# Seven block products instead of eight in part of a feed-forward input product, with PSUM kept as two tiles of four banks

## The chip, the cores and the metric

The kernel runs on one core of a Trainium2 chip, as one program. The metric is the device time of one execution in microseconds (us). The engines that matter are TensorE (PE in the profile; its weight loads are PEld), VectorE (DVE), ScalarE (ACT), and SyncE (SP), which issues the loads.

## The reference, cut to what matters

The model is a decoder trunk of two layers on 256 tokens with 2048 features, all in float32. Layer 0 has a recurrent block, layer 1 a sliding window attention, and each has a feed-forward part behind it:

```python
def swiglu_ffn(x, g, w_in, w_out):
    h = rms_norm(x, g)
    gate, up = jnp.split(h @ w_in, 2, axis=-1)
    return x + (jax.nn.silu(gate) * up) @ w_out
...
        if layer < N_REC:
            x = recurrent_block(x, norm1_g[layer], ...)
        else:
            if layer == N_REC:
                k_band, v_band = shared_kv(x, kv_norm_g, w_kv, k_norm_g)
            x = attn_block(x, norm1_g[layer], w_q[j], q_norm_g[j], sinks[j], w_o[j], k_band, v_band)
        x = swiglu_ffn(x, norm2_g[layer], ffn_w_in[layer], ffn_w_out[layer])
```

`w_in` of a feed-forward part (FFN) is 2048 x 11264 (gate and up, 5632 columns each), `w_out` 5632 x 2048.

## The kernel before

The residual stream `x` lies in SBUF for the whole program, with features on the 128 partitions and tokens in columns. All of the program is one stream of 704 chunks of weights (`stream`, L246). A chunk is 256 rows of a weight matrix by 512 of its columns, 128 partitions x 1024 numbers, 512 KB. At step i SyncE issues the load of chunk i + 4 into one of four buffers `raw`, chunk i + 3 is split, and the products of chunk i are issued.

A float32 product is made of three faster ones. `split` (L238) rounds a chunk to `hi` (ScalarE, L243) and takes the rest `lo` = raw − hi (VectorE, L244). Activations are split in the same way into a slot of 512 columns, 256 high and 256 low (there are 58 slots, L77). The products are hi x high, hi x low and lo x high.

`group` (L275) makes 512 output columns: four PSUM banks, one for each 128 columns, gather over all chunks of the group. `products` (L263, with the matmul on L271) issues 24 matmuls of 128x128 weights by 256 tokens for a chunk; in chunks 0, 2 and 5 (`SYNC`) three pairs of them are joined into matmuls of 512 columns, high and low side by side in the bank. The eight PSUM banks are eight tiles `b0` to `b7` (L83). `bank` (L163) takes one from the front of a queue, `free_bank` (L166) puts it at the back when its last read has been issued.

The order of the chunks, by number: 0 to 71 the input product and gates of the recurrent block in the order of `ORDER` (L53: x and y are groups of eight chunks, g is one chunk of gates, L547), 72 to 103 its output product, 104 to 279 the input product of FFN 0 (22 groups of 8), 280 to 367 its output product, 368 to 375 keys and values, 376 to 407 queries (L932, with tokens in rows), 408 to 439 the output product of the attention, 440 to 615 and 616 to 703 the two products of FFN 1. In the attention stage, work on heads is mixed among these chunks: scores (L783), their reads by a custom VectorE instruction (L794), transposes (L828, L906), values (L847).

What follows a group is issued by generator functions. `done` of a group reads its banks at once (`pull`, L306), tasks do the rest. `run_bg` (L194) steps the tasks at half a chunk, as long as an account of VectorE and ScalarE time (`self.dve`, `self.act`; each half tick takes 640 and 800 ns off) allows it. The helpers `a` (ScalarE, L107), `tt` (VectorE, L116) and `stt` (L120) record nearly all of these instructions, so their lines stand for many uses.

In `ffn` (L416) a group has 256 gate and 256 up columns. The product runs on x times the gain; the norm's factor `rstd` is multiplied on when the banks are read. A task then applies Silu, multiplies gate by up and splits the result into a slot `hid`, which `project` (L409) multiplies by `w_out`; `residual` (L387) adds the result to `x`.

## Time and profile before

| what | value |
|---|---|
| median of three runs | 2002.42 us (2001.57 to 2002.87) |
| the profiled execution | 2001.9 us |
| its span | 2000.1 us |
| TensorE busy, matmuls | 1991.9 us, 16509 instructions |
| VectorE busy | 1278.1 us, 2047 instructions |
| ScalarE busy | 1077.0 us, 1612 instructions |
| loaded from memory | 371.86 MB |

The profile is that of one execution. The span is the time from its first to its last instruction on the core. In rows of groups, out<-in names the tiles with their buffer numbers left out (`b` is any PSUM bank, `s` any slot, `h` a half buffer of 256 columns), then follow partitions x elements, the count, the busy time, the mean of one in ns, the idle time ahead of them and what ended it. Timeline rows have a start in us, a duration in us, engine, line, operation and count. A matmul's end is modelled; the starts are the better measure of what TensorE does.

### The profile page before, as it was taken

Reading aid. Unit: us, or ns where it says so; the run is one execution under the profiler, and the core shown is the slowest. Engines: PE = TensorE matmul, PEld = TensorE weight load, DVE = VectorE, ACT = ScalarE, POOL = GpSimd, SP = SyncE. Lnnn points to the kernel's source line nnn. Section 1 sums busy time; section 2 is a strip of 40 time slices with the busy share of each in tenths; the row PEclk is TensorE's granted clock in tenths of the full one; section 3 lists DMA queues with packets and bytes.
Section 4 is the critical chain, followed back from the end, with each engine's and each line's share of the span. In section 5 each row is a group of like instructions: output and inputs, shape, how many; then the busy total and the mean of one; then the engine's idle time right before and its main releaser. Section 6 shows DMA issues by size and latency. Waiting matters only on the chain. (4 is left out here: it accounts for less than half of the span.)

```text
span 2000.1 us, 39673 instructions
## 1 busy us (share of the span) xinstructions
PE 1991.9 (100%) x16509; PEld 1938.3 (97%) x16509; DVE 1278.1 (64%) x2047; ACT 1077.0 (54%) x1612; POOL 0.2 (0%) x4
## 2 busy tenths in 40 slices
PE   9999999999999999999999999999999999999999
PEld 9999999999999999999998789999999999999999
DVE  8989867556556655545677776765565566554443
ACT  7798655445445444444556775554454454444432
POOL 0000000000000000000000000000000000000000
PEclk9999999999999999999999999999999999999999
DMA  7554555555555555555554334555555555555553
GB/s 276 191 182 179 206 193 189 194 197 191 195 195 191 195 195 191 196 193 195 196 180 150 114 127 150 189 195 195 191 191 199 195 196 190 194 196 202 207 203 128
DMA packets 105012, 376.54 MB, mean 188 GB/s; under 512 B 11648, under 2 KB 13824, under 8 KB 104832
## 3 DMA queue, kind: packets, MB, share of 16 engines
q1 hardware_dynamic: 104544, 373.60, 52.3%
q8 instruction: 129, 2.11, 0.4%
q10 hardware_dynamic: 288, 0.40, 0.1%
q14 instruction: 51, 0.42, 0.1%
HBM read 371.86 MB, written 2.10 MB: 187 GB/s over the span
## 5 line engine op out<-in xcount | busy, mean ns | idle before, releaser
L271 PE MATMUL b<-s,hi 128*128 128x256 f32 (+1 forms) x9947 | 1356.4, 283 | 1.6 <-ACT s L107 1.2
L244 DVE TENSOR_TENSOR lo<-raw,hi 128x1024 fp32r<-128x1024 f32 (+1 forms) x705 | 860.9, 1222 | 669.1 <-ACT hi L243 666.1
L271 PEld LDWEIGHTS b<-s,hi 128*128 128x128 f32 x9947 | 1256.0, 188 | 26.2 <-ACT s L107 2.0
L243 ACT ACTIVATE hi<-raw 128x1024 fp32r<-128x1024 f32 (+1 forms) x705 | 746.1, 1059 | 773.0 <-PE b L271 728.1
L271 PE MATMUL b<-s,lo 128*128 128x256 f32 x5248 | 781.2, 276 | 0.0
L271 PEld LDWEIGHTS b<-s,lo 128*128 128x128 f32 x5248 | 680.7, 188 | 0.1
L932 PE MATMUL b<-hi,s 128*128 128x512 f32 x256 | 84.0, 408 | 0.0
L107 ACT ACTIVATE t<-b 128x256 f32<-128x256 f32 x122 | 45.9, 384 | 60.7 <-PE b L271 36.1
L932 PEld LDWEIGHTS b<-hi,s 128*128 128x128 f32 x256 | 45.8, 189 | 9.6 <-issue 1.4
L107 ACT ACTIVATE s<-b 128x256 fp32r<-128x256 f32 (+4 forms) x98 | 41.6, 465 | 19.5 <-PE b L828 7.9
L932 PE MATMUL b<-lo,s 128*128 128x512 f32 x128 | 50.8, 396 | 0.0
L107 ACT ACTIVATE h<-h 128x256 f32<-128x256 f32 (+1 forms) x104 | 38.9, 375 | 20.9 <-DVE h L116 20.8
L107 ACT ACTIVATE s<-h 128x256 fp32r<-128x256 f32 (+1 forms) x106 | 42.7, 413 | 13.1 <-DVE h L116 10.7
L116 DVE TENSOR_TENSOR h<-b,rstd 128x256 f32<-128x256 f32 x102 | 41.6, 415 | 0.0
L107 ACT ACTIVATE s<-x,par 128x256 fp32r<-128x256 f32 x80 | 37.8, 498 | 2.8 <-DVE x L116 1.8
L116 DVE TENSOR_TENSOR h<-h,rstd 128x256 f32<-128x256 f32 x92 | 38.3, 420 | 1.5
L107 ACT ACT_TABLE_LOAD x30 | 38.5, 1283 | 0.5
L116 DVE TENSOR_TENSOR h<-b,t 128x256 f32<-128x256 f32 x90 | 37.4, 417 | 0.0
L120 DVE SCALAR_TENSOR_TENSOR s<-x,par,s 128x256 fp32r<-128x256 f32 x80 | 36.5, 478 | 0.6 <-ACT s L107 0.6
L116 DVE TENSOR_TENSOR s<-h,s 128x256 fp32r<-128x256 f32 x88 | 36.6, 417 | 0.0
L116 DVE TENSOR_TENSOR h<-h,h 128x256 f32<-128x256 f32 x88 | 36.4, 415 | 0.0
L107 ACT ACTIVATE s<-s,h 128x128 f32<-128x128 f32 x64 | 28.3, 443 | 8.4 <-DVE h L125 8.2
(99 smaller groups left out, 690.3 us busy)
## 6 DMA issues: line engine op xcount, KB each, us to landing
raw<-in_ffn_in SPq DMA_DIRECT2D x352, 512.0 KB, 3.3
raw<-in_ffn_out SPq DMA_DIRECT2D x176, 512.0 KB, 3.2
raw<-in_lru_in SPq DMA_DIRECT2D x63, 512.0 KB, 3.8
raw<-in_lru_out SPq DMA_DIRECT2D x32, 512.0 KB, 3.5
raw<-in_w_q SPq DMA_DIRECT2D x32, 512.0 KB, 3.2
raw<-in_w_o SPq DMA_DIRECT2D x32, 512.0 KB, 3.4
raw<-in_gate SPq DMA_DIRECT2D x8, 512.0 KB, 4.0
raw<-in_kv SPq DMA_DIRECT2D x8, 512.0 KB, 3.2
```

Of the source, the lines that this page charges most:

```text
L107: self.nc.scalar.activation(out, in_, func, **kw)
L116: self.nc.vector.tensor_tensor(out, a, b, op)
L120: self.nc.vector.scalar_tensor_tensor(out, a, s, b, op0, op1)
L243: self.nc.scalar.activation(hi[:, q], raw[:, q], AF.Copy)
L244: self.nc.vector.tensor_tensor(lo[:, q], raw[:, q], hi[:, q].bitcast(F32), ALU.subtract)
L271: self.nc.tensor.matmul(ps[f][:, 0:c1 - c0], w, x2[k][:, c0:c1], start=f not in begun, stop=last and all(q[1] != f for q in todo[n + 1:]))
L932: nc.tensor.matmul(st[g][b][:, :], x, q, start=c + kt == 0 and x is xh and q is wh, stop=c == 7 and kt == 1 and q is wl)
```

## The change

**The seven products.** Seven of the 22 groups of each FFN input product (`FAST`: 5, 7, 9, 11, 13, 15, 17) are computed with tokens in rows: a chunk's 256 rows of features and its 256 + 256 columns make, with 2 x 128 tokens, a 2x2 by 2x2 product of blocks. In six chunks of eight (`PAIRS`) it is made from seven block products instead of eight, each of three matmuls (21 instead of 24) of 128 tokens by 256 columns. That needs combinations of the weights, which `mix` makes for each such chunk (ScalarE 768 + 1024 columns, VectorE 512, 256, 256, 768 and 1024), and combinations of the input, which are made once for each layer. Chunks 3 and 7 of such a group are plain; chunk 3 (`RUNS`) has nine matmuls of 512 columns and six of 256.

**The input.** The seven products are made on a normalized input `xn` (x times gain times `rstd`). Groups 0 to 3 (`PLAIN`) run as before on x times gain, and during them a background task `normed` makes `xn` and the combinations `mx`. The other groups run on `xn` in the old shape, mostly without the matmuls of 512 columns.

**Behind a group.** `joined` adds the seven products up (one ScalarE copy, five VectorE additions), applies Silu and multiplies. The result has tokens in rows; `turn` brings features back to the partitions by four transposes and a copy, at chunk 3 of the next fast group (`flush`). `direct` applies Silu and multiplies straight from PSUM for the other groups behind 3. The gated tiles stay unsplit, and a task `split`, started behind group 18, splits them.

**PSUM and SBUF.** PSUM is two tiles of four banks, `b0` and `b1`, whose banks are views. An FFN input group takes a whole tile (`bank4`), everything else takes single banks from the queue as before. SBUF has 30 double slots in place of 58 single ones, halved where a single one is needed, and four half buffers instead of eight. The columns of the FFN input weights are laid out as 256 up and 256 gate.

The diff, cut to its core:

```diff
+    PLAIN = 4
+    FAST = tuple(range(5, 18, 2))
+    PAIRS = (0, 1, 2, 4, 5, 6)
+    RUNS = 3
+    OWED = 9000.0
+    MORE = 2800.0
...
-        self.slots = deque(range(58))
+        self.whole = deque(range(30))
+        self.part = {F32: deque(), F32R: deque()}
...
-        self.banks = deque(psum.tile([P, 512], F32, name=f"b{i}") for i in range(8))
+        self.sets = []
+        for i in range(2):
+            b = psum.tile([P, 2048], F32, name=f"b{i}")
+            self.sets.append([b, [b[:, 512 * j:512 * j + 512] for j in range(4)]])
+        self.banks = deque(b for q in self.sets for b in q[1])
...
-        self.halves = deque(const.tile([P, T], F32, name=f"h{i}") for i in range(8))
+        self.halves = deque(const.tile([P, T], F32, name=f"h{i}") for i in range(4))
...
+    def bank4(self):
+        for q in self.sets:
+            if all(any(b is c for c in self.banks) for b in q[1]):
+                for b in q[1]:
+                    self.drop(b)
+                self.sets.remove(q)
+                self.sets.append(q)
+                return q
+        return [None, [self.bank() for _ in range(4)]]
+
+    def drop(self, b):
+        self.banks = deque(c for c in self.banks if c is not b)
...
+        if self.jobs[i][2]:
+            self.mix(i, raw, hi, lo)
+            return
...
+    def mix(self, i, raw, hi, lo):
+
+        act, tt = self.nc.scalar.activation, self.nc.vector.tensor_tensor
+        d = self.double(F32)
+        mh, ml = self.double(), self.double()
+        two = lambda ap: ap.rearrange("p (a c) -> p a c", c=T)
+        q = slice(T, 4 * T)
+        act(hi[:, q], raw[:, q], AF.Copy)
+        tt(two(d[:, 0:2 * T]), two(raw[:, T:3 * T]), raw[:, 0:T].unsqueeze(1).to_broadcast([P, 2, T]), ALU.subtract)
+        tt(d[:, 2 * T:3 * T], raw[:, 2 * T:3 * T], d[:, 0:T], ALU.add)
+        tt(d[:, 3 * T:4 * T], raw[:, 3 * T:4 * T], d[:, 2 * T:3 * T], ALU.subtract)
+        act(mh[:, :], d[:, :], AF.Copy)
+        tt(lo[:, q], raw[:, q], hi[:, q].bitcast(F32), ALU.subtract)
+        tt(ml[:, :], d[:, :], mh[:, :].bitcast(F32), ALU.subtract)
+        self.free(d)
+        self.mixed[i] = (mh, ml)
+        self.dve += self.MORE
...
+                    st["ps"] = self.bank4()[1] if four else [self.bank() for _ in range(4)]
...
+        def put(h, x, w, n=1):
+            b = h // 2
+            nc.tensor.matmul(st["ps"][0][:, h * T:(h + n) * T], x, w, start=b not in st["begun"], stop=True,
+                             skip_group_check=True)
+            st["begun"].add(b)
...
+            if c == self.RUNS:
+                n = narrow(wide[3]) + narrow(wide[4]) + narrow(wide[5])
+                todo = sum(map(full, wide[0:3]), []) + n[0:1] + sum(map(full, wide[6:9]), []) + n[1:2]
+                todo += sum(map(full, wide[9:12]), []) + n[2:]
+            else:
+                todo = sum(map(narrow, wide), [])
...
+            part = lambda s, q: (s[:, q * P:q * P + P], s[:, T + q * P:T + q * P + P])
+            com = lambda q: (m[:, q * P:q * P + P], m[:, 2 * T + q * P:2 * T + q * P + P])
+            old = lambda q: (hi[:, q * T:q * T + T], lo[:, q * T:q * T + T])
+            new = lambda q: (mh[:, q * T:q * T + T], ml[:, q * T:q * T + T])
+            todo = ((5, part(a, 0), old(1)), (3, part(b, 0), old(3)), (2, com(3), old(2)),
+                    (7, com(0), new(0)), (6, com(2), new(1)), (4, com(1), new(2)), (1, part(b, 1), new(3)))
+            for n, (h, (xh, xl), (wh, wl)) in enumerate(todo):
+                if n == 4:
+                    self.half_tick()
+                put(h, xh, wh)
+                put(h, xl, wh)
+                put(h, xh, wl)
...
+                if c == self.RUNS:
+                    self.flush()
+                (fast if c in self.PAIRS else plain)(c, hi, lo)
...
+            def joined(q, g=g):
+                ps, banks = q
+                p1, c, u, h = self.half(), self.double(F32), self.slot(F32), self.slot(F32)
+                b = two(c[:, :])
+                twice = lambda ap: ap.unsqueeze(1).to_broadcast([P, 2, T])
+                at = lambda i, n=1: ps[:, i * T:(i + n) * T]
+                self.a(p1, at(5))
+                self.tt(b[:, 0:4:3, :], two(at(3, 2)), twice(p1), ALU.add)
+                self.tt(two(u), two(at(6, 2)), twice(c[:, 3 * T:4 * T]), ALU.add)
+                self.tt(c[:, 3 * T:4 * T], at(7), u[:, 0:T], ALU.add)
+                self.tt(c[:, T:3 * T], at(1, 2), u, ALU.add)
+                self.tt(c[:, 3 * T:4 * T], at(0), c[:, 3 * T:4 * T], ALU.add)
+                for p in banks:
+                    self.free_bank(p)
+                self.a(c[:, 0:2 * T], c[:, 0:2 * T], AF.Silu)
+                self.tt(h, c[:, 2 * T:4 * T], c[:, 0:2 * T], ALU.mult)
+                self.free_half(p1)
+                self.free(c)
+                self.free(u)
+
+                def turn():
+                    p = self.mbank()
+                    for j in range(2):
+                        for i in range(2):
+                            nc.tensor.transpose(p[:, j * T + i * P:j * T + i * P + P],
+                                                h[:, i * T + j * P:i * T + j * P + P],
+                                                self.con[:, K_ID:K_ID + P])
+                    s = self.slot(F32)
+                    self.a(s, p)
+                    self.free_mbank(p)
+                    self.free(h)
+                    raw(g, s)
+                self.pend.append(turn)
...
+            if g < self.PLAIN:
+                self.group(src, ND, xs, start, g == self.PLAIN - 1, self.SYNC, four=True)
+            elif g in self.FAST:
+                self.fast_group(src, xn, mx, g, joined, g == self.FAST[-1])
+            else:
+                end = g == self.FAST[-1] + 1
+                self.group(src, ND, xn, direct, g == NH // 2 - 1, (0, 3, 4, 5) if end else (), True, 3 if end else None)
+            if g == 0:
+                def begin(n=len(self.jobs) - 8):
+                    self.spawn(normed())
+                    self.DEBT = self.OWED
+                self.jobs[-8] = self.with_(self.jobs[-8], begin)
...
-        wi = np.asarray(ffn_w_in)[l].reshape(D, 2, NH, P).transpose(0, 2, 1, 3).reshape(D, 2 * DFF)
+        wi = np.asarray(ffn_w_in)[l].reshape(D, 2, NH // 2, 2 * P)[:, ::-1].transpose(0, 2, 1, 3).reshape(D, 2 * DFF)
```

What this does to the order of instructions, at three places.

TensorE in the recurrent block, where the second group (x1) ends and the third (x2) begins, with the waits of each instruction; `s0` holds the first input slot of x2's first chunk. Before:

```order
L271 MATMUL b0_83<-s14_206,hi3_78 128x256 x2
L271 MATMUL b0_83<-s14_206,lo3_82 128x256
L271 MATMUL b0_83<-s15_225,hi3_78 128x256 x2
L271 MATMUL b0_83<-s15_225,lo3_82 128x256
L271 MATMUL b2_85<-s0_150,hi0_75 128x256 [waits Activation_49]
L271 MATMUL b2_85<-s0_150,hi0_75 128x256
L271 MATMUL b3_86<-s0_150,hi0_75 128x256 x2
L271 MATMUL b4_87<-s0_150,hi0_75 128x256 x2
L271 MATMUL b1_84<-s0_150,hi0_75 128x256 x2
```

After:

```order
L355 MATMUL b0_83<-s7_189,hi3_78 128x256 x2
L355 MATMUL b0_83<-s7_189,lo3_82 128x256
L355 MATMUL b0_83<-s0_140,hi0_75 128x256 [waits DVE_49,Activation_49]
L355 MATMUL b0_83<-s0_140,hi0_75 128x256 x9
L355 MATMUL b1_84<-s0_140,hi0_75 128x256 [waits DVE_49,Activation_49]
L355 MATMUL b1_84<-s0_140,hi0_75 128x256 x3
```

Before, the group x2 waits for its weights alone, and its banks are other tiles than those that x1 has just filled. Now its first product goes to the tile `b0` that x1's last products went to, and it waits for VectorE's read of that tile; the first product into `b1` waits for a read of `b1`.

TensorE in the attention stage: the scores of one head pair (L783 before, L1075 after) among the products of the queries (L932 before, L1224 after). Before:

```order
L932 MATMUL b6_89<-hi2_77,s49_11212 128x512 x2
L932 MATMUL b6_89<-lo2_81,s49_11212 128x512
L783 MATMUL b3_86<-s30_11093,s53_11620 128x128 [waits Activation_49]
L783 MATMUL b3_86<-s30_11093,s53_11620 128x128
L783 MATMUL b3_86<-s30_11093,s53_11620 128x256 x2
L783 MATMUL b4_87<-s30_11093,s53_11620 128x128 x2
L783 MATMUL b4_87<-s30_11093,s53_11620 128x256 x2
L932 MATMUL b5_88<-hi2_77,s55_11230 128x512 x2
L932 MATMUL b5_88<-lo2_81,s55_11230 128x512
```

After:

```order
L1120 MATMUL b1_84<-con_65,s21_11809 128x128
L1075 MATMUL b1_84<-s14_11259,s3_11831 128x128 x2
L1075 MATMUL b1_84<-s14_11259,s3_11831 128x256 x2
L1224 MATMUL b0_83<-hi1_76,s26_11429 128x512 [waits DVE_49]
L1224 MATMUL b0_83<-hi1_76,s26_11429 128x512
L1224 MATMUL b0_83<-lo1_80,s26_11429 128x512
```

Before, the products of the queries go on into `b5` without a wait. Now they go into a bank of `b0`, and wait for VectorE, which reads the scores in another bank of `b0`.

VectorE in the input product of FFN 0. Before, between two groups' splits (L244) stand the reads of banks, the products with `rstd` and the split of the gated tile:

```order
L244 TENSOR_TENSOR lo1_80<-raw1_72,hi1_76 128x1024
L244 TENSOR_TENSOR lo2_81<-raw2_73,hi2_77 128x1024
L116 TENSOR_TENSOR h4_99<-b6_89,t3_94 128x256
L116 TENSOR_TENSOR h4_99<-h4_99,rstd1_104 128x256
L116 TENSOR_TENSOR h5_100<-b7_90,t0_91 128x256
L116 TENSOR_TENSOR h6_101<-b0_83,rstd1_104 128x256
L116 TENSOR_TENSOR h5_100<-h5_100,rstd1_104 128x256
```

After, in the chunks ahead of the first fast group (L309 is the plain split, L319 to L321 the combinations `d`, L323 and L324 the rests of the weights and of `d`):

```order
L319 TENSOR_TENSOR s19_5190<-raw0_71 128x512
L320 TENSOR_TENSOR s19_5190<-raw0_71,s19_5190 128x256
L309 TENSOR_TENSOR lo2_81<-raw2_73,hi2_77 128x1024
L321 TENSOR_TENSOR s19_5190<-raw0_71,s19_5190 128x256
L319 TENSOR_TENSOR s15_5225<-raw1_72 128x512
L320 TENSOR_TENSOR s15_5225<-raw1_72,s15_5225 128x256
L324 TENSOR_TENSOR s28_5192<-s19_5190,s4_5191 128x1024
L309 TENSOR_TENSOR lo3_82<-raw3_74,hi3_78 128x1024
```

The five instructions of a fast chunk stand among the plain splits, and the plain split of the chunk ahead of them is issued between the combinations.

207 lines of the change are left out of this document (180 added, 27 removed).

## Prediction

> **What bounds the kernel now.** I read the page first, for the span, the engines' shares and the granted clock.
>
> ```profile
> span 2000.1 us, 39673 instructions
> PE 1991.9 (100%) x16509; PEld 1938.3 (97%) x16509; DVE 1278.1 (64%) x2047; ACT 1077.0 (54%) x1612; POOL 0.2 (0%) x4
> PEclk9999999999999999999999999999999999999999
> ```
>
> TensorE is busy from end to end at the full clock, so one product less is worth its slot on TensorE, and one wait of TensorE costs its full length. The profiled execution took 2001.9 us, 1.8 us around its span of 2000.1 us; the sum below is made against 2001.9, and the median of the runs, 2002.42, lies 0.5 us above it. About 0.2% (4 us) is what a measurement of this kernel tells from no change.
>
> Then the busy time by stage: recurrent block up to its output product, first FFN with its end, its output product, the attention stage with the end of FFN 0, second FFN, last product. Columns are the window, its length, then busy time of PE, PEld, DVE, ACT, POOL, the clock, the DMA share and GB/s.
>
> ```profile
> 7.00:298.00 291.00, 289.59 (x2455) 285.77 (x2454) 250.02 (x456) 219.49 (x375) 0.00 (x0) 1.00 0.57 204
> 298.00:777.00 479.00, 479.00 (x4023) 470.82 (x4022) 292.67 (x404) 239.13 (x315) 0.00 (x0) 1.00 0.54 194
> 777.00:1017.00 240.00, 240.00 (x2084) 238.52 (x2083) 131.79 (x158) 110.18 (x136) 0.00 (x0) 1.00 0.54 194
> 1017.00:1274.00 257.00, 254.60 (x1788) 223.97 (x1787) 191.52 (x492) 170.71 (x373) 0.00 (x0) 1.00 0.41 146
> 1274.00:1753.00 479.00, 479.00 (x4021) 470.79 (x4020) 293.14 (x406) 238.97 (x315) 0.00 (x0) 1.00 0.54 194
> ```
>
> In the FFN input windows VectorE works 61% and ScalarE 50% of the time: the added weight combinations have room on average. In the recurrent block VectorE works 86%, so whatever must wait for a read by it there waits in a full queue. The loads take about half of the DMA engines, and their number and size don't change (704 blocks of 512 KB), so I cost them at nothing; a TensorE that waits only gives them more time.
>
> TensorE's waits between 1040 and 1240 us, the attention stage, are these and no others (total, times, longest):
>
> ```profile
> PE b L828 <- DVE s L125: 0.8, 3, 0.3
> PE b L783 <- ACT s L107: 0.7, 1, 0.7
> PE b L271 <- ACT s L107: 0.5, 1, 0.5
> PE b L847 <- ACT s L107: 0.3, 1, 0.3
> ```
>
> So 2.3 us in 200 us: today eight PSUM tiles are enough for TensorE to go on while scores and probabilities are read.
>
> **The products removed.** The timeline of TensorE in the first FFN gives the slot of one product.
>
> ```profile
> 701.88 1.98 PE L271 MATMUL b<-s,hi 128*128 128x256 f32 x16
> 703.70 1.07 PE L271 MATMUL b<-s,lo 128*128 128x256 f32 x8
> 704.60 1.98 PE L271 MATMUL b<-s,hi 128*128 128x256 f32 x13
> ```
>
> A chunk's 24 products take 704.60 − 701.88 = 2.72 us, 113.4 ns each. A fast chunk has 21 (seven block products, three each). Two layers, seven fast groups, six fast chunks of eight: 84 chunks, 252 products fewer, 252 × 0.1134 = 28.6 us off. I take the same slot for the new shape, since it is also 128x128 stationary by 256 moving columns.
>
> **The transposes added.** Fourteen gated tiles come out with tokens in rows and are turned by four 128x128 transposes each. The same form in the queries:
>
> ```profile
> 1069.86 0.60 PE L906 MATMUL b<-con,s 128*128 128x128 f32 x4
> 1070.21 0.71 PE L932 MATMUL b<-hi,s 128*128 128x512 f32 x2
> ```
>
> The next product starts 0.35 us after the first transpose: 14 × 0.35 = 4.9 us on. Products and transposes together: −23.7 us.
>
> **The work of VectorE and ScalarE.** The groups by form, mean ns of one behind the busy time:
>
> ```profile
> L244 DVE TENSOR_TENSOR lo<-raw,hi 128x1024 fp32r<-128x1024 f32 x703 | 859.5, 1223 | 665.3 <-ACT hi L243 662.3
> L243 ACT ACTIVATE hi<-raw 128x1024 fp32r<-128x1024 f32 x703 | 744.8, 1060 | 771.3 <-PE b L271 728.1 <-ACT s L107 13.5 <-PE b L932 12.5
> L244 DVE TENSOR_TENSOR lo<-raw,hi 128x512 fp32r<-128x512 f32 x2 | 1.4, 692 | 3.8 <-ACT hi L243 3.8
> L116 DVE TENSOR_TENSOR h<-b,t 128x256 f32<-128x256 f32 x90 | 37.4, 417 | 0.0
> L107 ACT ACTIVATE s<-b 128x384 f32<-128x384 f32 x32 | 14.5, 487 | 7.9 <-PE b L828 7.9
> L107 ACT ACTIVATE s<-b 128x512 fp32r<-128x512 f32 x16 | 9.4, 587 | 2.8 <-PE b L906 2.7
> ```
>
> A fast chunk costs VectorE 0.692 + 2 × 0.417 (combinations) + 0.957 (768 wide, halfway between 512 and 1024) + 1.223 = 3.71 us against 1.22 now; ScalarE 0.82 (768, halfway again) + 1.06 = 1.88 us. A fast group takes TensorE 6 × 21 + 2 × 24 = 174 slots, 19.7 us, and VectorE 6 × 3.71 + 2 × 1.22 = 24.7 us: more than TensorE. But each fast group stands beside a plain one: 21.8 us of TensorE with 9.8 us of splits and about 0.8 of multiplications, and the joining of the seven products (five additions, one multiplication, some 3.5 us). The pair takes VectorE 38.8 us, TensorE 41.5. VectorE may run three chunks ahead (8 us), and that lead covers the 5.0 us by which a fast group overruns. I take 0 here; if the cover is gone, that is the second rival. ScalarE's 6 × 1.88 + 2 × 1.06 = 13.4 us stays under 19.7. The normalized input (sixteen gains, splits, 48 half-width combinations) is some 25 us of VectorE against 87 us of four plain groups whose splits need 39: hidden. Splitting gated tiles later moves them under groups 19 to 21, where nothing else is due: nothing.
>
> **The wait that the change adds.** The diff makes two PSUM tiles of four banks out of eight of one, and the built program keeps its waits per tile: as its order shows, a product into one bank of a set now waits for a VectorE or ScalarE instruction that reads another. Groups of the FFN input product take whole sets in turn, and there the reader has a whole group's time. Everywhere else single banks are taken. Counted in the order: products that wait for a read which itself needs a product at most some 0.7 us of TensorE work earlier. Before: none in the recurrent block and 9 in the attention stage, on data or the same bank. After: 21 in the recurrent block, 7 in its output product, 59 in the attention stage. What is queued behind each is all of TensorE.
>
> In the recurrent block, first from one group to the next:
>
> ```profile
> 53.82 0.28 PE L271 MATMUL b<-s,lo 128*128 128x256 f32 x1
> 53.93 1.98 PE L271 MATMUL b<-s,hi 128*128 128x256 f32 x16
> 55.08 0.75 DVE L116 TENSOR_TENSOR s<-b,rstd 128x256 f32<-128x256 f32 x2
> ```
>
> The next group starts at 53.93; the old banks are read until 55.83, 1.9 us later. Now it starts only after such a read. Behind the sigmoids:
>
> ```profile
> 78.41 1.98 PE L271 MATMUL b<-s,hi 128*128 128x256 f32 x16
> 79.34 1.57 ACT L107 ACTIVATE s<-b,par 128x256 f32<-128x256 f32 x4
> ```
>
> The group starts at 78.41, the four sigmoids run 79.34 to 80.91, the third to about 80.5 (2.1 us late). Prices: seven waits on a third bank, with seven products as cover, 0.1 us (0.1 to 0.5); four on a last bank, with one or none, 1.2 (0.7 to 1.9, as late as in the trace); eight pairs of sigmoids 1.0 (0.35, one read after another, to 2.5); the output product and the norm 0.8 together (0.5 to 1.1). Sum: 0.7 + 4.8 + 8.0 + 0.8 = 14.3 us; ends 6.8 and 32.2.
>
> In the attention stage:
>
> ```profile
> 1073.09 1.08 PE L783 MATMUL b<-s,s 128*128 128x128 f32 x8
> 1074.01 0.64 PE L932 MATMUL b<-hi,s 128*128 128x512 f32 x2
> 1075.45 0.41 DVE L794 CUSTOM_DVE_ANT_0 s<-b,con,par 128x128 f32<-128x128 f32 x1
> 1077.05 0.08 DVE L794 DVE_READ_ACCUMULATOR2_ANT h<- 128x1 f32 x1
> ```
>
> Scores end at 1074.17, the queries' products have gone on since 1074.01, and the scores are read from 1075.45 to 1077.13, 1.68 us long and starting 1.28 us late. After the change these products go into the same set and wait for the read. Thirteen waits of this kind at about the read itself: 13 × 1.6 = 21 us. Of the other 46, nine are the old ones; 37 are copies of 384 or 512 by ScalarE or 256-wide reads by VectorE, 0.42 to 0.59 us long, plus 0.16 for the end of the product (a product ends 0.28 after its start, its slot is 0.11): 0.65 each, 24 us. Sum 45 us. Lower end: only score reads, 21 us. Upper end: each score read behind one split (1.68 + 1.22 = 2.9) and the others at 1.0 with half a split ahead: 13 × 2.9 + 37 = 75 us. I take the middle, near the read's own row, because VectorE is free a quarter of the time in this stage.
>
> [...]
>
> **Slower slots.** In part of the recurrent block a chunk takes longer:
>
> ```profile
> 161.86 2.05 PE L271 MATMUL b<-s,hi 128*128 128x256 f32 x16
> 163.74 1.10 PE L271 MATMUL b<-s,lo 128*128 128x256 f32 x8
> 164.69 2.04 PE L271 MATMUL b<-s,hi 128*128 128x256 f32 x16
> ```
>
> That is 2.83 us, 0.11 more. New waits may bring more of it: 2 us (0 to 6).
>
> **Sum.** −28.6 + 4.9 + 14.3 + 45 + 2 = +37.6: 2001.9 + 37.6 = 2039.5, and 2040.0 on the scale of the median. Ends: −23.7 + 6.8 + 21 = +4.1, 2006; −23.7 + 32 + 75 + 6 = +89, 2091.
>
> **The rivals.** First, the waits are covered and the change is faster. The place is the attention stage and the recurrent block: if the readers come at once and the waiting products find the set free, only the removed products count: 2001.9 − 23.7 = 1978 us. It decides when all new waits stay under 23.7 − 4 = 19.7 us. For it: VectorE is free a quarter of the attention stage, and two waits in a row can share one read. Against it: the score reads alone, 1.68 us long with next to no product between, make 21. Chance 0.12, of it 0.08 faster and 0.04 (waits of 20 to 28 us) within 0.2%.
>
> Second, VectorE becomes the bound in the fast groups. If its lead doesn't cover the overrun, because the joining and the combinations stand ahead of splits in its queue, each fast group ends up to 5.0 us late: 14 × 5.0 = 70 us on top, 2110. Against it: 38.8 us of 41.5 per pair. Chance 0.06.
>
> Third, the FFN input product falls into the slow slots, since the plain groups from 4 on have none of the 512-wide products that groups have now in three chunks: 15 groups × 8 chunks × 0.11 × 2 layers = 26 us, 2066 with the rest. For it: 161.86 shows that slots can be slow. Against it: chunk 3 of each fast group keeps nine such products, and no FFN window is slow now. Chance 0.08. The forecast itself has 0.74.
>
> **How the numbers follow.** 2040 is the forecast's own time. The range starts at 2006, where the lowest prices meet, and ends at 2080, short of 2091 since not all upper ends meet at once; it holds the third rival and leaves out the first, the second and the forecast's edge: under 0.2. Faster 0.08 and same 0.04 are the first rival's; the rest, 0.88, is slower.
>
> **What would show it.** In the new profile the two FFN input windows should be about 12 us shorter each (23.7 over two layers) with hardly a wait of TensorE in them; the attention stage some 45 us longer, with waits of TensorE for the score reads leading its list; the recurrent block and its output product some 14 us longer. The prediction is wrong if TensorE's waits outside the FFN sum to under 20 us, if TensorE waits for the second part of the weights or for the combinations in fast chunks, or if a chunk of 24 products in plain groups takes clearly over 2.72 us.

## The result, and the profile after

The changed kernel takes 2086.27 us (median of four runs, 2081.39 to 2087.65) against 2002.26: a ratio of 1.0415, interval 1.0397 to 1.0433. The forecast was slower, 2040 us with a range from 2006 to 2080. The sign and the main mechanism, waits of TensorE outside the FFN input products, came out; the size did not. The profile is of the fastest of the four runs (2081.39 us).

The page of the changed kernel, its first lines:

```profile
span 2079.5 us, 39947 instructions
PE 2008.3 (97%) x16487; PEld 1944.6 (94%) x16487; DVE 1458.9 (70%) x2291; ACT 1124.6 (54%) x1629; POOL 0.2 (0%) x4
```

TensorE was busy for all but 8 us of the span before; now 71 us are idle, and it is busy for 16 us longer with fewer products. The busy time by stage tells where (recurrent block with its output product, FFN 0 input, its output, keys to attention output, FFN 1 input, its output; columns as in the prediction). Of before, cut at the same chunks, and of after:

```profile
7.00:298.30 291.30, 289.89 (x2457) 286.00 (x2456) 250.32 (x457) 219.79 (x375) 0.00 (x0) 1.00 0.57 204
298.30:778.20 479.90, 479.90 (x4032) 471.78 (x4031) 293.53 (x406) 239.53 (x316) 0.00 (x0) 1.00 0.54 193
1018.10:1277.80 259.70, 257.30 (x1808) 226.54 (x1807) 193.63 (x496) 171.78 (x376) 0.00 (x0) 1.00 0.41 147
```

```profile
7.00:324.60 317.60, 300.30 (x2448) 293.24 (x2446) 251.23 (x453) 225.65 (x377) 0.00 (x0) 0.99 0.53 187
324.60:799.30 474.70, 473.96 (x4022) 468.86 (x4023) 383.06 (x534) 260.97 (x326) 0.00 (x0) 1.00 0.56 196
1038.70:1360.80 322.10, 275.40 (x1808) 231.77 (x1808) 199.07 (x500) 173.64 (x377) 0.00 (x0) 0.97 0.33 119
1360.80:1835.50 474.70, 474.04 (x4022) 468.96 (x4023) 381.38 (x530) 259.30 (x323) 0.00 (x0) 1.00 0.55 195
```

The recurrent block and its output product take 26.3 us more, the attention stage 62.4, each FFN input product 5 us less. The rest makes 1 us, and the sum is the 79.4 us between the two spans. In the attention stage the granted clock (the share of full speed that TensorE was given) is 0.97, where it was 1.00.

TensorE's longest waits in the attention stage now, where the list of before summed to 2.3 us:

```profile
PE b L1120 <- DVE s L138: 9.5, 5, 3.9
PE b L1224 <- ACT s L120: 7.0, 6, 3.0
PE b L1224 <- DVE h L1086: 5.7, 8, 1.0
PE b L355 <- ACT s L120: 4.3, 4, 1.6
PE b L355 <- ACT t L120: 3.8, 4, 1.3
```

The queries' products (L1224) do wait for the score reads (L1086), as forecast, but at most 1.0 us each. The longest waits are others. The first row is transposes (L1120) that wait for the last multiplication of a softmax; the same kind of wait took 0.8 us in the list of before (L828 behind L125). One of the second row, 3.05 us, on the timeline:

```profile
1200.83 1.28 ACT L120 ACT_TABLE_LOAD   x1 [3.24 <-DVE h L129]
...
1202.12 0.40 ACT L120 ACTIVATE s<-s,h 128x128 f32<-128x128 f32 x1
...
1203.49 0.49 ACT L120 ACTIVATE s<-s,h 128x256 f32<-128x256 f32 x1
...
1203.98 0.57 ACT L120 ACTIVATE s<-b 128x512 fp32r<-128x512 f32 x1
...
1204.61 1.22 PE L1224 MATMUL b<-hi,s 128*128 128x512 f32 x2 [3.05 <-ACT s L120]
```

TensorE waits for a copy of 0.57 us out of PSUM. The copy stands in ScalarE's queue behind a table load and four exponentials of a softmax, 3.2 us of work (1200.83 to 1203.98) that has nothing to do with that bank. This wait cost what was queued ahead of the reader, 3.05 us, not only the read.

The same in the recurrent block, behind a chunk of gates. ScalarE and then TensorE:

```profile
83.40 1.28 ACT L120 ACT_TABLE_LOAD   x1
84.70 1.57 ACT L120 ACTIVATE s<-b,par 128x256 f32<-128x256 f32 x4
```

```profile
85.95 2.72 PE L355 MATMUL b<-s,hi 128*128 128x256 f32 x16 [2.42 <-ACT s L120]
88.47 1.91 PE L355 MATMUL b<-s,lo 128*128 128x256 f32 x8
90.18 2.28 PE L355 MATMUL b<-s,hi 128*128 128x256 f32 x16
```

The table load stands ahead of the sigmoids, and the next group starts 2.42 us late. After that its 16 products take 2.72 us where 1.98 is usual: the wait has a second price. The windows around it show which (the clock is the third column from the end):

```profile
80.00:83.50 3.50, 3.50 (x29) 3.25 (x28) 3.22 (x7) 3.13 (x6) 0.00 (x0) 1.00 0.42 157
83.50:86.00 2.50, 0.08 (x2) 0.05 (x1) 2.50 (x8) 2.49 (x5) 0.00 (x0) 1.00 0.55 210
87.40:90.70 3.30, 3.30 (x17) 3.30 (x17) 2.36 (x5) 2.65 (x6) 0.00 (x0) 0.50 0.37 130
```

About 1.3 us after the idle stretch (83.53 to 85.95) the clock falls to half for 3.4 us (87.28 to 90.70), which costs 1.7 us. Five such stretches in this execution, two of them twice as long, make 23.9 us. TensorE was busy in 21.9 of them, so they cost some 10.9 us, 9.2 of it in the attention stage.

In the fast groups hardly anything waits, but a fast chunk takes 2.46 us (447.90 to 450.36) in place of the 2.38 of my sum:

```profile
447.90 0.40 PE L509 MATMUL b<-hi,s 128*128 128x256 f32 x2
...
448.94 1.58 PE L509 MATMUL b<-s,s 128*128 128x256 f32 x12
450.36 0.40 PE L509 MATMUL b<-hi,s 128*128 128x256 f32 x2
```

The nine products with plain weights take 1.04 us, 116 ns each, the twelve with combined weights 1.42 us, 118 ns each.

### The profile page after: what moved, and what is told of

Read it like the earlier page. It is cut to its first block, busy times and chain, and to the rows that moved or that the text cites. A ratio compares the mean times of both kernels' runs of the same rounds, so it can differ in the third digit from the quotient of the medians.

```text
span 2079.5 us, 39947 instructions
## 1 busy us (share of the span) xinstructions
PE 2008.3 (97%) x16487; PEld 1944.6 (94%) x16487; DVE 1458.9 (70%) x2291; ACT 1124.6 (54%) x1629; POOL 0.2 (0%) x4
## 5 line engine op out<-in xcount | busy, mean ns | idle before, releaser
L355 PE MATMUL b<-s,hi 128*128 128x256 f32 (+1 forms) x8455 | 1135.5, 281 | 22.6 <-ACT s L120 12.0
L355 PEld LDWEIGHTS b<-s,hi 128*128 128x128 f32 x8455 | 1054.9, 188 | 40.5 <-ACT s L120 14.6
L309 DVE TENSOR_TENSOR lo<-raw,hi 128x1024 fp32r<-128x1024 f32 (+1 forms) x621 | 755.2, 1220 | 450.2 <-ACT hi L308 447.3
L355 PE MATMUL b<-s,lo 128*128 128x256 f32 x4352 | 650.4, 277 | 0.0
L355 PEld LDWEIGHTS b<-s,lo 128*128 128x128 f32 x4352 | 567.1, 188 | 0.2 <-ACT s L120 0.2
L509 PE MATMUL b<-hi,s 128*128 128x256 f32 (+1 forms) x868 | 163.0, 292 | 0.0
L509 PEld LDWEIGHTS b<-hi,s 128*128 128x128 f32 x868 | 130.4, 189 | 3.8
L509 PE MATMUL b<-s,s 128*128 128x256 f32 x1008 | 133.3, 281 | 0.0
L509 PEld LDWEIGHTS b<-s,s 128*128 128x128 f32 x1008 | 125.2, 189 | 0.0
L324 DVE TENSOR_TENSOR s<-s,s 128x1024 fp32r<-128x1024 f32 x84 | 102.7, 1222 | 20.8 <-ACT s L322 20.0
L509 PE MATMUL b<-lo,s 128*128 128x256 f32 (+1 forms) x434 | 114.1, 289 | 0.0
L1224 PE MATMUL b<-hi,s 128*128 128x512 f32 x256 | 88.0, 426 | 15.4 <-ACT s L120 7.0
L323 DVE TENSOR_TENSOR lo<-raw,hi 128x768 fp32r<-128x768 f32 x84 | 79.4, 951 | 0.0
L1224 PEld LDWEIGHTS b<-hi,s 128*128 128x128 f32 x256 | 46.0, 195 | 30.7 <-ACT s L120 9.0
L319 DVE TENSOR_TENSOR s<-raw 128x512 f32<-128x512 f32 x84 | 57.7, 687 | 11.5 <-DMA raw<-in_ffn_in 11.0
```

The source lines that it names most:

```text
L309: self.nc.vector.tensor_tensor(lo[:, q], raw[:, q], hi[:, q].bitcast(F32), ALU.subtract)
L319: tt(two(d[:, 0:2 * T]), two(raw[:, T:3 * T]), raw[:, 0:T].unsqueeze(1).to_broadcast([P, 2, T]), ALU.subtract)
L323: tt(lo[:, q], raw[:, q], hi[:, q].bitcast(F32), ALU.subtract)
L324: tt(ml[:, :], d[:, :], mh[:, :].bitcast(F32), ALU.subtract)
L355: self.nc.tensor.matmul(ps[f][:, 0:c1 - c0], w, x2[k][:, c0:c1], start=f not in begun, stop=last and all(q[1] != f for q in todo[n + 1:]))
L509: nc.tensor.matmul(st["ps"][0][:, h * T:(h + n) * T], x, w, start=b not in st["begun"], stop=True, skip_group_check=True)
```

## The experiments

The theory from here on: two PSUM tiles of four banks make TensorE wait for reads of other banks, and this is the whole loss outside the FFN input products. The rival: the new accounts of background work, the debt of 9000 ns and four half buffers delay the readers, whatever the tiles.

**Eight tiles.** The change with PSUM as before, and the two additions across banks made bank by bank:

```diff
-            b = psum.tile([P, 2048], F32, name=f"b{i}")
...
+        self.banks = deque(psum.tile([P, 512], F32, name=f"b{i}") for i in range(8))
...
-                self.tt(b[:, 0:4:3, :], two(at(3, 2)), twice(p1), ALU.add)
+                self.tt(b[:, 0, :], at(3), p1, ALU.add)
+                self.tt(b[:, 3, :], at(4), p1, ALU.add)
```

> The changed kernel with PSUM as eight tiles of one bank again; the sums of two banks in the joining are made by one instruction for each bank; all else as changed. Theory (waits by set of four banks): the recurrent block, its output product, and the attention stage come back to their times of before (207.0, 84.4 and 236.2 us for queries and output product), the granted clock is 1.00 throughout, and only the gain of about 10 us in the two FFN input products stays: 1992 us (1987 to 1998). Rival (the new accounts of background work, the larger debt of 9000 ns and the four half buffers delay the readers, whatever the tiles): the attention stage stays 40 us or more longer than before, 2050 us or more.

Measured: 1987.94 us (ratio 0.9932 to before, 0.9919 to 0.9944), 98 us less than the changed kernel, and 0.7% faster than the kernel before. Recurrent block, attention and an FFN input product in its profile:

```profile
7.00:299.00 292.00, 290.20 (x2452) 286.01 (x2452) 250.39 (x455) 219.66 (x375) 0.00 (x0) 1.00 0.62 204
1011.90:1270.30 258.40, 255.51 (x1808) 226.02 (x1808) 193.16 (x496) 171.65 (x376) 0.00 (x0) 1.00 0.45 148
1270.30:1743.20 472.90, 472.90 (x4019) 468.16 (x4018) 383.51 (x545) 262.02 (x323) 0.00 (x0) 1.00 0.60 196
```

Both stages are back at 292.0 and 258.4 us, with the clock at 1.00, under the same accounts, debt and buffers. The rival falls.

**The kernel before with two tiles.** The other way round: only the PSUM tiles of the change, and whole tiles for FFN input groups.

```diff
-        self.banks = deque(psum.tile([P, 512], F32, name=f"b{i}") for i in range(8))
+            b = psum.tile([P, 2048], F32, name=f"b{i}")
+            self.sets.append([b, [b[:, 512 * j:512 * j + 512] for j in range(4)]])
+        self.banks = deque(b for q in self.sets for b in q[1])
...
-                    st["ps"] = [self.bank() for _ in range(4)]
+                    st["ps"] = self.bank4()[1] if four else [self.bank() for _ in range(4)]
```

> The kernel before with one thing of the change, PSUM as two tiles of four banks, taken whole by FFN input groups and bank by bank elsewhere. Theory (waits by set): the recurrent block with its output product is some 26 us longer, the attention stage some 60 us, the FFN stages are as before: 2002 + 88 = 2090 us (2075 to 2100), with the granted clock at 0.5 in some stretches of the attention stage. Rival (accounts and buffers): no change, 2002 us.

Measured: 2097.30 us, ratio 1.0473 (1.0457 to 1.0489), 95 us on top. Recurrent block, FFN 0 input left out, and attention stage:

```profile
7.00:325.50 318.50, 301.55 (x2450) 295.09 (x2449) 250.93 (x455) 225.38 (x377) 0.00 (x0) 0.99 0.56 186
1046.20:1366.20 320.00, 272.87 (x1807) 234.87 (x1805) 198.16 (x496) 173.42 (x375) 0.00 (x0) 0.96 0.36 119
```

Without one product of the new scheme the recurrent block takes 27 us more and the attention stage 60, as in the changed kernel (26 and 62). Cause and place are shown from both sides.

**Eight tiles, no fast group.** What the seven products are worth by themselves.

```diff
-    FAST = tuple(range(5, 18, 2))
-    PAIRS = (0, 1, 2, 4, 5, 6)
+    FAST = ()
+    PAIRS = ()
```

> Eight tiles as in the first, and no fast group: all FFN input groups behind the first four run in the old shape on the normalized input, no combinations are made. It tells what the seven products are worth. By the trace of the changed kernel a fast group takes 20.81 us with its transposes and a plain one 21.76: 14 x 0.95 = 13 us above the first kernel, 2005 us, so about the time before. By my sum (slots of 113.4 ns, 0.35 us for transposes) it would be 23.7 us above. If the combinations held TensorE up, it would not be slower than the first kernel.

Measured: 2001.42 us, 0.9996 to before (0.9987 to 1.0005). The seven products gain 13.5 us, as read from the trace of the changed kernel, and not the 23.7 of my sum. So the combinations do not hold TensorE up.

**Where the slower slots of fast chunks come from**, in two kernels: the moving operand of the twelve products from `hi` and `lo`, and the stationary one from there.

```diff
-            new = lambda q: (mh[:, q * T:q * T + T], ml[:, q * T:q * T + T])
+            new = old
```

> Eight tiles as in the first; the four block products of a fast chunk that use weight combinations read the plain high and low parts of the weights instead (the combinations are still made, but not used, so the output is not the FFN's). It tells where the slower slots of the fast chunks come from. If they come from where the moving operand lies (a slot of the pool instead of hi or lo), the 12 products take 113.4 ns each instead of 118 to 120, a fast chunk 2.38 us instead of 2.46, and the time falls by 84 x 0.07 = 6 us. If they come from the order of the products or from VectorE's and ScalarE's load, nothing changes.

```diff
-                    (7, com(0), new(0)), (6, com(2), new(1)), (4, com(1), new(2)), (1, part(b, 1), new(3)))
+                    (7, sta(2), new(0)), (6, sta(3), new(1)), (4, sta(4), new(2)), (1, sta(5), new(3)))
```

> Eight tiles; in the four block products of a fast chunk that use weight combinations, the stationary operand is read from the plain weights (hi, lo) instead of the input combinations, the moving operand stays the weight combinations (so the output is not the FFN's). It tells whether the slower slots, 118 to 120 ns, come with the moving operand alone or with both operands lying in slots of the pool. If with both: the 12 products take 113.4 ns in the first three chunks of a fast group, as they did when the moving operand was read from hi and lo (7.15 us for 63 products instead of 7.41). If the moving operand alone does it: 7.4 us as in the first kernel.

Measured: 1998.06 us and 1987.43 us (one run). With the moving operand from `hi` and `lo` the first three chunks take 7.15 us, 113.5 ns a product, as expected, in 12 of 14 groups (7.42 us in the other two). The time did not fall by the 6 us that I expected, because from the transposes in chunk 3 on all products are slow, through the whole plain group behind it:

```profile
429.46 2.05 PE L344 MATMUL b<-s,hi 128*128 128x256 f32 x16
431.35 1.10 PE L344 MATMUL b<-s,lo 128*128 128x256 f32 x8
432.29 1.93 PE L344 MATMUL b<-s,hi 128*128 128x256 f32 x15
```

That is 2.83 us a chunk, where eight tiles alone has 2.72, and it makes the kernel 10 us slower. With the stationary operand changed, the three chunks take 7.36 us instead of 7.41: the twelve products go from 118.7 to 116.6 ns, and the nine with plain weights from 116.3 to 117.0. So in the sum the moving operand mattered (113.5 ns a product against 118.7) and the stationary one hardly (7.36 us against 7.41); and slow slots went on here where both are as in plain groups.

**Another order of the seven products, and an older moving operand.**

```diff
-            todo = ((5, part(a, 0), old(1)), (3, part(b, 0), old(3)), (2, com(3), old(2)),
-                    (7, com(0), new(0)), (6, com(2), new(1)), (4, com(1), new(2)), (1, part(b, 1), new(3)))
+            todo = ((5, part(a, 0), old(1)), (7, com(0), new(0)), (3, part(b, 0), old(3)), (6, com(2), new(1)),
+                    (2, com(3), old(2)), (4, com(1), new(2)), (1, part(b, 1), new(3)))
```

> The first kernel with the seven block products of a fast chunk in another order, those with plain and with combined weights in turn. It tells whether the slower slots need several such products in a row. If so: 84 chunks x 0.05 us = 4 us faster than the first kernel, 1984 us. If each such product is slow by itself: no change, 1988 us.

```diff
-            new = lambda q: (mh[:, q * T:q * T + T], ml[:, q * T:q * T + T])
+            new = lambda q: (m[:, q * T:q * T + T], m[:, 3 * T - q * T:4 * T - q * T])
```

> Eight tiles; the four block products of a fast chunk that use weight combinations read their moving operand from the input combinations, which lie in slots of the pool as well but were written long before (the output is not the FFN's). It tells whether the slower slots of the fast chunks come with where the moving operand lies, or with its having just been written (a wait for it stands between the products). If with the place: 7.4 us for the first three chunks of a group, as in the first kernel. If with the waits: 7.15 us.

Measured: 1989.47 us (0.9937, interval 0.9925 to 0.9950) and 7.40 us for three chunks, no change; and 1993.04 us (one run) with 7.41 us. Of the 5 us that this run has over eight tiles, 1.7 are a stretch at half clock and some 3 slower slots in plain groups of FFN 1. In turn, the twelve products take 117.3 ns and the nine 117.5. For the time of a chunk neither the order nor the moment of writing mattered (7.40 and 7.41 us against 7.41); what is left is where the moving operand lies. But plain groups also move from slots of the pool, at 113 ns, so the place alone does not explain it either.

**Four tiles of two banks**, the dose between.

```diff
+        two = [psum.tile([P, 1024], F32, name=f"b{i}") for i in range(4)]
+        self.two = [[b[:, 512 * j:512 * j + 512] for j in range(2)] for b in two]
+        self.banks = deque(b for q in self.two for b in q)
```

> The first kernel with PSUM as four tiles of two banks; FFN input groups take two whole tiles. By the order, 36 products wait for a read that ends shortly ahead of them (86 with two tiles, 15 with eight). Theory (each such wait costs about its read, some 1.0 us in all, and long idle stretches halve the clock for a while): 21 waits more than with eight tiles, 20 to 30 us, 2013 us (2003 to 2025); the idle stretches are shorter, so the granted clock stays at 1.00 or close to it. Rival (the waits cost nothing by themselves, and the loss with two tiles came from the lower clock after long stretches alone): within 4 us of the first kernel, 1988 us.

Measured: 2020.39 us, ratio 1.0091 (1.0075 to 1.0106), 32.5 us above eight tiles. Recurrent block and attention stage:

```profile
7.00:307.30 300.30, 296.75 (x2452) 291.19 (x2451) 251.11 (x456) 219.26 (x374) 0.00 (x0) 1.00 0.59 198
1019.90:1303.30 283.40, 269.64 (x1811) 231.54 (x1810) 196.58 (x499) 172.81 (x378) 0.00 (x0) 0.98 0.41 135
```

The waits cost by themselves, so the rival falls. The clock did not stay at 1.00: its low stretches cost 6.4 us. The other 26 us over 21 waits would be 1.2 us each, but they are not all idle time: against eight tiles, TensorE is idle for 12.6 us more in the two windows (17.3 against 4.7), and slower slots in the recurrent block and its output product (116.9 and 115.6 ns against 115.0 and 113.6) make 4.9 us.

**Added waits.** Twenty waits put into TensorE's work in the FFN output products:

```diff
+                if nk == NH and c in (5, 11, 17) and self.gaps:
+                    self.gap(self.gaps.popleft())
```

> The first kernel with 20 idle stretches put into TensorE's work in the two FFN output products: after a chunk's products TensorE waits for a chain of 2 to 14 VectorE additions of 256 columns, 0.33 us each. It tells from which length on an idle stretch lowers the granted clock, and what that costs. Theory: a stretch of some 2.5 us or more is followed by one or two stretches of 3.4 us at half clock, which cost 1.7 us each; below some 2 us nothing but the stretch itself is lost. Rival: the clock answers to the share of idle time over a longer time, and single stretches up to 5 us leave it at 1.00.

Each wait needs two added products: one that VectorE reads (L343), and one that waits for the chain (L347). The second was issued later than I had placed it, so the idle stretches came out at 0.3 to 0.5 us, and the question about the clock stays unanswered here. Yet the kernel took 2018.04 us (one run), 30 us more than eight tiles. TensorE around the first pair:

```profile
786.03 1.98 PE L358 MATMUL b<-s,hi 128*128 128x256 f32 x13
787.85 1.07 PE L358 MATMUL b<-s,lo 128*128 128x256 f32 x8
788.76 0.28 PE L343 MATMUL b<-zero 128*128 128x256 f32 x1
788.88 2.05 PE L358 MATMUL b<-s,hi 128*128 128x256 f32 x16
790.76 0.40 PE L358 MATMUL b<-s,lo 128*128 128x256 f32 x2
791.22 0.38 PE L347 MATMUL b<-gz,zero 128*128 128x256 f32 x1
791.44 0.87 PE L358 MATMUL b<-s,lo 128*128 128x256 f32 x6
792.15 2.05 PE L358 MATMUL b<-s,hi 128*128 128x256 f32 x16
794.03 1.10 PE L358 MATMUL b<-s,lo 128*128 128x256 f32 x8
794.97 2.05 PE L358 MATMUL b<-s,hi 128*128 128x256 f32 x16
```

Before it the work of 16 products (three pairs joined, so 13 instructions) takes 1.82 us (786.03 to 787.85), behind L343 it takes 1.88 (788.88 to 790.76), ahead of any wait; a chunk takes 2.82 us (792.15 to 794.97) in place of 2.72, and this goes on for 16 chunks, until the next group. So one product of another kind, for which TensorE waited for nothing, was enough here to start the slower slots: the mean slot went from 113.3 to 117.8 ns at L343 in all eight cases in which it was 113.3 ahead of it. At L347 the slower slots ended in two of 20 cases (954.59 and 1003.76 us). A wait did so too: in the recurrent block and its output product of the changed kernel, all three waits that found TensorE at 113.3 left it at 117.8 (55.8, 168.9 and 278.6 us). 69% and 84% of the products of the two stages were slow here, none with eight tiles alone: 14.5 of the 30 us. To see whether the runs of 512-wide products end it, I moved them:

```diff
+            runs = (0, 6, 12, 18) if nk == NH else self.SYNC
```

> The kernel with 20 added waits again (they came out as short ones, 0.3 to 0.6 us of idle time), with the chunks of the FFN output products that hold matmuls of 512 columns moved to right behind each wait (chunks 0, 6, 12, 18 in place of 0, 2, 5). Theory (a short wait puts TensorE into slots of 118 ns, and only a run of 512-wide products brings 113 back): the slow slots end in the chunk behind each wait, their share in the two stages falls from 0.69 and 0.84 to under 0.2, and the time falls from 2018 to about 2006 us. Rival (the slower slots come from the added instructions' load on VectorE or end by themselves): no change, 2018 us.

Measured: 2017.93 us (one run), no change; 91% and 53% of the products were slow. Of the 22 runs of 512-wide products that met slow slots, 3 ended them; in the kernel before this, with runs in chunks 0, 2 and 5, it was 4 of 6. In part the waiting product still stood behind the run of its chunk. My theory of what ends it falls, and with it that only waits start it.

**Runs of 512 columns in the recurrent block.**

```diff
-done, sync=self.SYNC if g == 1 else ())
+done, sync=self.SYNC if g else ())
...
-done, g == 3, self.SYNC if g == 1 else ())
+done, g == 3, self.SYNC if g else ())
```

> The kernel with eight tiles, with the matmuls of 512 columns in chunks 0, 2 and 5 of all groups of the recurrent block behind the first ones (g over 0), in place of g = 1 alone. There the slow slots have a share of 0.38 of the products, worth 1689 x 1.7 ns = 2.9 us. Theory of the slots: up to 2.9 us faster than with eight tiles alone, 1985 us, less what the added reads of both bank halves cost on VectorE and ScalarE, which are nearly full there. Rival: these reads come late and TensorE waits for them: 1990 us or more.

Measured: 1988.52 us (0.9931, 0.9917 to 0.9944), as with eight tiles alone. By the starts of TensorE's products the recurrent block was 0.5 us shorter and its output product 0.2 us; the share of slow products fell only from 0.37 to 0.29. The stage of `w_o` was 1.7 us longer, which is a stretch of 3.4 us at half clock (from 1188.0 us) that the profile of eight tiles alone has not. So neither the theory's 2.9 us nor the rival's late reads came.

**Long waits.**

```diff
+        for _ in range(k):
+            self.nc.scalar.activation(hi[:, 0:512], raw[:, 0:512], AF.Copy)
```

> Eight tiles; at 20 chunks of the two FFN output products ScalarE writes half of the high part of the weights 16 to 23 times more than needed (0.5 us each), so that it comes late and TensorE has one idle stretch of some 1 to 4 us, the only one for 8 chunks. It tells which single stretch lowers the granted clock, and what that costs. Theory, from the idle stretches of the changed kernel (2.42 us lowered it at 83.5 us and not at 113.3): stretches over some 2.2 us halve the clock for 3.4 us more often than not, at 1.7 us each; stretches under 1.7 us never do. Rival: what counts is how busy TensorE is over tens of us; then single stretches leave the clock at 1.00 up to 4 us.

The stretches came out longer than meant, all but one 4.3 to 9.7 us, and the kernel took 2178.23 us (one run). Each of these 19 brought half clock. The first of them, the stretch and what follows:

```profile
791.30:795.40 4.10, 0.00 (x0) 0.00 (x0) 1.23 (x1) 4.00 (x6) 0.00 (x0) 0.92 0.54 151
795.40:801.00 5.60, 5.50 (x25) 5.50 (x26) 1.23 (x1) 1.08 (x2) 0.00 (x0) 0.50 0.48 172
802.00:808.00 6.00, 6.00 (x54) 6.00 (x53) 2.37 (x3) 2.12 (x2) 0.00 (x0) 1.00 0.49 155
```

Stretches of 4.3 to 7.1 us brought 6.8 us at half clock, those of 7.9 to 9.7 us 10.2 us (one of 4.4 us brought 3.4). The half clock often began before the stretch ended, by up to 6.3 us, and while TensorE was idle it cost nothing; TensorE was busy in 2.9 to 6.1 us of it, which cost 1.4 to 3.1 us a stretch. Of the 190 us over eight tiles, 128 are the stretches and some 42 the half clock behind them. A single stretch was enough here; the rival falls. What happens between 1 and 4 us, these stretches do not tell, but the other profiles do. In three kernels with waits for sets (the changed kernel, the kernel before with two tiles, four tiles), cut into rows of 1 us over most of the recurrent block and the attention stage, stretches of 2.2 to 2.6 us lowered the clock in 6 of 8 cases (in the changed kernel 2.42 us did at 83.53 us and did not at 113.33 us); under 1.4 us none did that stood alone. With eight tiles a single wait of 1.7 us in the attention stage left it at 1.00 (the first kernel), and one of 1.80 us (from 1287.02 us, in the kernel of these long waits) lowered it. 1.64 us with four tiles (from 1190.42 us) did it too, so the theory's "under 1.7 us never" falls.

The place of a stretch made a difference too. In the profile of the changed kernel the five low stretches start at 87.28, 1135.18, 1148.83, 1203.44 and 1281.95 us, which is 307, 4, 16 and 23 times 3.413 us apart. Cut at these distances into windows, this profile shows half clock behind all five windows at full clock in which TensorE was idle for 2.08 us or more, and behind none of 47 with 0.52 to 1.68 us. The stretch of 2.42 us at 113.33 us is split between two windows, 1.27 and 1.15 us of idle time, and the clock stays at 1.00:

```profile
111.20:114.60 3.40, 2.13 (x19) 1.93 (x17) 3.40 (x8) 3.37 (x6) 0.00 (x0) 1.00 0.24 83
114.60:118.00 3.40, 2.25 (x19) 2.25 (x20) 3.32 (x7) 3.33 (x9) 0.00 (x0) 1.00 0.33 127
```

That at 83.53 us has 2.1 of its 2.42 us in one window, which ends at 87.3 us, where the clock falls. The kernel before with two tiles has a stretch of 3.21 us (from 1366.08 us) that left the clock at 1.00, and the 1.64 us with four tiles were followed by half clock from 1192.48 us: what was enough in one kernel was not in another, and the five and the 47 give no limit for other kernels. That the windows decide is a reading of these traces and is not shown: no kernel here moved a wait against them.

## Why the prediction was right in sign and wrong in size

- **The wait by set** was right. It is shown by eight tiles, which takes the loss away, and by the kernel before with two tiles, which has it without the rest of the change. The first rival, waits that are covered, did not come; the kernel with eight tiles, which has hardly any waits, takes 1988 us where this rival had 1978.
- **The prices of the waits** were too low in the recurrent block, and in the attention stage their sum came near by luck. Of the 26.3 us in the recurrent block and its output product, 1.7 are the clock and 6.2 slower slots (mean slot 117.2 against 114.8 ns over 1728 products, 116.1 against 113.4 over 768), so the waits are 18.4 against 14.3. The row of the table load at 78.05 us was on the timeline of before and I left it out: the sigmoids were late by 2.1 us because of it, and I took 1.0. In the attention stage 62.4 less 9.2 of clock leaves 53 against 45. The score reads were to lead the list at 21 us and made 8.5 in 11 waits; copies behind a softmax cost up to 3 us where I had 0.65; and the transposes' waits for the softmax, among the old waits to which I gave no price, grew from 0.8 to 9.5 us.
- **The clock** had no term in the sum: 10.9 us. The step that failed is "one wait of TensorE costs its full length": behind waits came half clock (10.9 us) and, in the recurrent block and its output product, slower slots (6.2 us) as well. The profile of before has the clock at 1.00 throughout and could not show it.
- **The slots** failed at "I take the same slot for the new shape": 20.38 us for a fast group without its transposes where the sum has 19.7, 14 x 0.65 = 9 us. The transposes took 0.35 us, as taken. The term of 2 us for slower slots should have been 6 in the recurrent block and its output product alone.
- **The range** ended 6 us short, because I had cut its end from 2091 to 2080; 2091 would have held the time by luck, since neither end had a term for the clock or for the slots of the fast groups. The other three runs lie 4 to 6 us above the profiled one; their granted clock was 0.991 to 0.992 against 0.994, which I estimate at as much. By stages the miss of 41.8 us in the profiled run is 10.0 in the recurrent block, 17.4 in the attention stage, 13.4 in the FFN input products and 1.0 elsewhere.
- **The second rival**, VectorE as the bound, did not come: its busy time in an FFN input window went from 293.5 to 383.1 us of 474.7 and TensorE waits in the first of them for 0.9 us in all. **The third**, slow plain groups, did not come either in the changed kernel; it did in the kernel whose moving operands came from `hi` and `lo`. Its price was wrong too: plain groups from 4 on are 11 in a layer (22 less groups 0 to 3 less the seven of `FAST`), not 15, so 19 us and not 26.

What stays open is what decides between slots of 113 and 118 ns. Here three waits of the changed kernel and eight added products started the longer slots; with the moving operand in `hi` and `lo` the twelve products took 113.5 ns in place of 118.7; what ends them I could not find. With four tiles the attention stage is 25.0 us longer than with eight; idle time makes 10.9 and the clock 6.4 of it, and the cause of the other 7.7 stays open too.

## What to carry to other kernels

Where a framework keeps its waits by tile, a PSUM tile should hold only what is written and read together; joining eight tiles to two saved two additions in each fast group and cost 95 to 98 us. Price a wait of TensorE by the queue of the engine that it waits for, table loads and all, and then add the second price: in the changed kernel four of the five waits of 2.4 to 3.9 us were followed by 3.4 to 6.8 us at half clock, with four tiles one of 1.64 us was too, and a wait of 1.93 us (at 55.79 us) moved the slots from 113.3 to 117.8 ns. A saving in product count is worth the slots that the new products take, so look for the slot of the new form before multiplying.

## What the runs showed of the hardware that I had not expected

- An added product for which nothing waits moved TensorE from 113.3 to 117.8 ns a product in eight of eight cases; with the other added products behind it, this went on for up to 18 chunks of 24 products.
- In the changed kernel one idle stretch of 2.42 us (at 83.53 us) was followed, 1.3 us after its end, by 3.4 us at half clock, and another of 2.42 us (at 113.33 us) was not. The starts of its five low stretches lie whole multiples of 3.413 us apart; cut by them, the first stretch has 2.1 us in one window, the second 1.27 and 1.15 us in two.
- Twelve products whose moving operand is the combined weights take 118.7 ns each in a row; with another order or another stationary operand they take 117.3 or 116.6 ns, but the products beside them slow down, and the chunk takes nearly as long as before (7.40 and 7.36 us for three chunks, against 7.41).
